# Maxima of the grouped-query scores from the keys' high parts, two stretches of keys at once in the two halves of TensorE's rows

## The chip, the cores and the metric

One Trainium2 chip, one of its cores. The metric is device time in microseconds of one execution of the whole program, two layers of it. The kernel before was timed in 3 runs.

## What is computed

Two layers of a token mixer over 256 context and 2048 latent tokens. Each layer projects the normalised input and runs four branches side by side: A differential attention (two softmax maps per head), B grouped-query attention, C a chunked gating MLP, D gated linear attention; the gated results go through one output projection. The change touches branch B alone: 4 query heads of width 64 share 2 key and value heads.

```python
def gqa_core(q, k, v):
    s = jnp.einsum('bqhgd,bkhd->bhgqk', q, k).astype(jnp.float32) * (GQ_HD ** -0.5)
    p = jax.nn.softmax(s, axis=-1)
    return jnp.einsum('bhgqk,bkhd->bqhgd', p.astype(v.dtype), v)
```

The latent queries read all 2304 keys. The context queries, in the first layer only, read the 256 context keys.

## The kernel before

**Stages.** In each layer the projections for A and B come first, then those of C and D with D's scans, then the attention of A and B together with the gates' projection, then the output projection. Only the attention (lines 789 to 1124) is touched.

**Split operands.** Queries and keys of both attentions lie in DRAM as a high and a low part, so that two or three products of the fast format give nearly the product of full precision. For B the tile `ka` (line 840) holds the 64 rows of a key head's high part interleaved with the 64 of its low part, and `kb` (line 843) the high part again in partitions 0 to 63 and ones in 64 to 127, written by GpSimd. On the query's side `qa` (line 871) holds each row of the high part twice, and `qb` (line 873) the low part in partitions 0 to 63 and, in 64 to 127, what is added to every score of a query: the negated maximum of its row. One product of `ka` with `qa` and one of `kb` with `qb` then give the score less the maximum.

**Blocks.** A block is 256 latent queries (two tiles `qt` of 128) of head r in both A and B; there are 32 in a layer. Keys are cut into 3 chunks of 768. A block makes 12 chunks of A's scores (`da_chunk`, line 901: two matmuls of 384 columns into the two banks of a tile `s`, of which there are two), which VectorE copies out with a running minimum (line 906). Then come the 6 chunks of B's maxima (`g_chunk`, lines 937 to 949): two matmuls of 384 columns (line 940), all 128 rows of `qa` against `ka`, and a pass of VectorE (line 945) that keeps only the running minimum of the negated scores, in the end in column 64 of a zeroed tile `mz`. `qb()` (line 951) transposes `mz` and ScalarE copies 64 partitions of it into `qb`. After that B's scores are computed once more, transposed (`gs`, lines 974 and 975), and go through the exponential into `gp` (line 977). `tr` (line 962) transposes A's weights into `wt`. `pvm` (line 996) multiplies both with the values: `gp` into output partitions 64 to 127, `wt` into 0 to 63, so that the two matmuls of a pair use different halves of TensorE's columns. These come in three groups a block.

**Order.** TensorE's order is the program's own. Every piece of a block has a slot and a priority (`S.at`, lines 1031 to 1071), and `S.run` writes the pieces out slot by slot. The second half of a block (`tr`, `gs`, `pvm`, `o1` to `o3`) lies in the slots of the next block's chunks. Into every slot `pace.fill` puts some matmuls of the gates' projection (`pz`, line 1161), by count, not by time. In a slot the order is: chunk, `tr`, `pace.fill`, `gs`, `pvm`, `pace.fill`.

**Loads.** All loads are issued by SyncE in the program's order. `ld_ka` loads `ka` and then `kb` for one chunk of keys (lines 841 and 844), for every second head; `qload` loads a block's queries, `qa` and `qb` among them (lines 872 and 876).

Of the kernel before, what the change touches and what calls it, by code (L numbers as in the profile page):

```python
# [9 lines left out]
F32 = mybir.dt.float32  # L10
# [10 lines left out]
P = 128  # L21
# [83 lines left out]
class Kernel:  # L105
# [683 lines left out]
    def attention(self, i, out):  # L789
        tc, nc, D = self.tc, self.nc, self.D[i]  # L790
# [8 lines left out]
        with ExitStack() as cx:  # L799
# [6 lines left out]
            sp = cx.enter_context(self.pool(f"sp{i}", 4))  # L806
# [3 lines left out]
            mz = []  # L810
# [8 lines left out]
            def rows(name, r0, cs, dims):  # L819

                a = D[name][r0, 0, cs]
                return bass.AP(tensor=a.tensor, offset=a.offset, ap=[[d * NT, n] for d, n in dims] + [list(a.ap[-1])])
# [12 lines left out]
            def ld_ka(R, c):  # L835
                if R["h"] % 2:
                    return
                r0 = 256 + 64 * (R["h"] // 2)
                cs = slice(c * CH, (c + 1) * CH)
                t = kp.tile([P, CH], F32R, name="ka", tag="ka", bufs=4)  # L840
                nc.sync.dma_start(out=t.bitcast(F32), in_=rows("bqk", r0, cs, [(1, 128)]))
                R["KA"].append(t)
                t = kp.tile([P, CH], F32R, name="kb", tag="kb", bufs=4)
                nc.sync.dma_start(out=t[0:64, :].bitcast(F32), in_=rows("bqk", r0, cs, [(2, 64)]))
                nc.gpsimd.memset(t[64:128, :].bitcast(F32), 1.0)
                R["KB"].append(t)

            def ld_v(R, b):
# [7 lines left out]
            def new_round(r, prev):  # L856
                if r % 2:
                    return dict(h=r, dak=[[], []], V=[], KA=prev["KA"], KB=prev["KB"])
                return dict(h=r, dak=[[], []], V=[], KA=[], KB=[])

            def qload(R, q0):
                h = R["h"]
                ctx = "c" if q0 == 0 else ""
                bufs = 1 if q0 == 0 else 3
                qs = slice(q0, q0 + 256)
                daq = []
                for m in range(2):
                    t = qp.tile([P, 256], F32R, name=f"daq{m}", tag=f"daq{m}{ctx}", bufs=bufs)
                    nc.sync.dma_start(out=t.bitcast(F32), in_=rows("aqk", (2 * h + m) * 32, qs, [(0, 2), (1, 64)]))
                    daq.append(t)  # L870
                QA = qp.tile([P, 256], F32R, name="qa", tag="qa" + ctx, bufs=bufs)
                nc.sync.dma_start(out=QA.bitcast(F32), in_=rows("bqk", h * 64, qs, [(2, 64), (0, 2)]))
                QB = qp.tile([P, 256], F32R, name="qb", tag="qb" + ctx, bufs=bufs)
                a = D["bqk"][h * 64, 1, qs]
                src = bass.AP(tensor=a.tensor, offset=a.offset, ap=[[2 * NT, 64], list(a.ap[-1])])
                nc.sync.dma_start(out=QB[0:64, :].bitcast(F32), in_=src)
                return dict(daq=daq, QA=QA, QB=QB)

            def block(R, Q, q0, nk, base):
                full = nk == NT  # L880
                ch = CH if full else nk
                nch = NCH if full else 1
                hc = ch // 2
                nkt = nk // P
                nu = nkt // 2
                h = R["h"]
# [49 lines left out]

                def g_chunk(qt, c):
                    s = pf.tile([P, 2, 512], F32, name="s", tag="s")
                    for u in range(2):
                        nc.tensor.matmul(  # L940
                            s[:, u, :hc], lhsT=Q["QA"][:, qt * P : (qt + 1) * P],
                            rhs=R["KA"][c][:, u * hc : (u + 1) * hc], start=True, stop=True,
                        )
                    nm = sp.tile([P, 1], F32, name="gm", tag="gm", bufs=6) if c < nch - 1 else mz[qt][:, 64:65]
                    nc.vector.tensor_scalar(  # L945
                        out=junk[:, :ch].rearrange("p (u f) -> p u f", u=2), in0=s[:, :, :hc], scalar1=-1.0,
                        scalar2=GM.get(qt, BIG), op0=ALU.mult, op1=ALU.min, accum_out=nm,
                    )
                    GM[qt] = nm

                def qb():
                    t = pb.tile([P, 512], F32, name="b", tag="b")
                    for qt in range(2):
                        nc.tensor.transpose(t[:, qt * P : (qt + 1) * P], mz[qt], ident)
                    nc.scalar.copy(Q["QB"][64:128, :], t[64:128, :256])

                def tr(u):
                    s = pb.tile([P, 512], F32, name="b", tag="b")
# [72 lines left out]
                s, step = (base, 1) if full else (base + 0.25, 2)  # L1031
# [12 lines left out]
                for c in range(nch):  # L1044
                    for qt in range(2):
                        S.at(s, lambda qt=qt, c=c: g_chunk(qt, c), 0)
                        s += step
                S.at(s + 1, qb, 8)
                b0 = s + 2
                if full:  # L1050
# [26 lines left out]
            base = 0  # L1077
            R = new_round(0, None)
            Qs = {0: qload(R, blocks[0][1])}
            for c in range(NCH):  # L1080
                ld_dak(R, c)
            ld_ka(R, 0)
            pace.begin()
            for c in range(1, NCH):
                ld_ka(R, c)
            for c in range(2):
                S.at(6 + 4 * c, lambda c=c, R=R: ld_v(R, c), 8)
            for bi, (r, q0) in enumerate(blocks):
                if with_ctx and bi % 8 == 0:
                    block(R, qload(R, 0), 0, NCTX, base)  # L1090
                end = block(R, Qs[bi], q0, NT, base)
                Rx = R
                if bi + 1 < len(blocks):
                    if blocks[bi + 1][0] != r:
                        Rx = new_round(r + 1, R)
                        for c, z in enumerate((-14, -10, -8)):
                            S.at(end + z, lambda c=c, Rx=Rx: ld_dak(Rx, c), 8)
                        for c, z in enumerate((-8, 8, 13.5)):
                            S.at(end + z, lambda c=c, Rx=Rx: ld_ka(Rx, c), 8)
                        for c, z in enumerate((-8, 18)):  # L1100
                            S.at(end + z, lambda c=c, Rx=Rx: ld_v(Rx, c), 8)

                    def pre(bi=bi, Rx=Rx):
                        Qs[bi + 1] = qload(Rx, blocks[bi + 1][1])

                    S.at(base + 1, pre, 8)
                S.run(end)
                R = Rx
                base = end
# [355 lines left out]
```

## Time and profile before

| what | value |
|---|---|
| median of 3 runs | 3940.55 us (3936.79 to 3941.91) |
| profiled execution, its own time | 3940.16 us |
| its span, first to last instruction | 3938.4 us |
| PE busy | 3687.3 us (94%) |
| PE weight loads busy | 3078.7 us (78%) |
| VectorE (DVE) busy | 2675.3 us (68%) |
| ScalarE (ACT) busy | 2212.4 us (56%) |
| GpSimd (POOL) busy | 1171.5 us (30%) |
| granted TensorE clock, mean | 0.970 |

PE is TensorE's matmul side and PEld its weight loads, which run beside the matmuls. A matmul's recorded duration reaches from its start to the end of its way through the array; matmuls behind one another overlap, so what one costs is the distance from its start to the next one's. A granted clock of 1.00 is 2.4 GHz, 0.5 is 1.2 GHz.

### The profile page before, as it was taken

What the parts mean: (1) busy time and instruction counts of PE and PEld (TensorE: products, weight loads), DVE (VectorE), ACT (ScalarE), POOL (GpSimd) and SP (SyncE); (2) the same over time, 40 slices, a digit from 0 to 9 for tenths busy, and PEclk for the clock granted to TensorE, in tenths of its full rate; (3) what the DMA queues carried; (4) which work ended last, traced back from release to release, by engine and by line L of the source; (5) the groups of instructions that cost most, each with busy time, mean ns of one, the idle gap of its engine ahead of it and who ended that gap; (6) DMA issues with size and microseconds to landing.
All of it is one profiled execution on the core that took longest, in us unless ns stands there. A gap on an engine that the chain in (4) does not pass through costs nothing.

```text
span 3938.4 us, 71719 instructions
## 1 busy us (share of the span) xinstructions
PE 3687.3 (94%) x25908; PEld 3078.7 (78%) x25908; DVE 2675.3 (68%) x6264; ACT 2212.4 (56%) x4508; POOL 1171.5 (30%) x1328
## 2 busy tenths in 40 slices
PE   7999997999998999998989999979999999999798
PEld 4888885787887888876778878868878778888576
DVE  5555444887787877866666544458777778887575
ACT  4433443666666666665544434436666666666564
POOL 0223222233333333333312222213333333333332
PEclk8999998999999999999999999989999999999899
DMA  7655444534335343326556542254342432432443
GB/s 272 198 172 179 139 151 127 154 107 135 111 100 151 104 121 101 104 85 225 183 178 206 177 144 91 93 142 123 96 138 91 126 115 92 121 100 87 147 163 117
DMA packets 407524, 537.73 MB, mean 137 GB/s; under 512 B 107832, under 2 KB 271616, under 8 KB 407168
## 3 DMA queue, kind: packets, MB, share of 16 engines
q1 hardware_dynamic: 407168, 533.14, 43.1%
q8 instruction: 205, 3.36, 0.4%
q14 instruction: 151, 1.24, 0.1%
HBM read 395.63 MB, written 137.32 MB: 135 GB/s over the span
## 4 chain that ended last, share of the span: by engine, by line
PE 74%; DVE 9%; DMA 7%; ACT 5%; issue 3%; SPq 1%; POOL 1%; DVEq 0%; ACTq 0%; POOLq 0%
PE pv L996 12%; PE pz L1161 8%; PE b L962 6%; PE s L901 6%; PE b L974 4%; PE s L940 3%; PE b L975 3%; PE po L139 2%; PE po L141 2%; PE po L140 2%; DVE e L906 2%; PE pc L139 2%; PE pc L140 2%; PE pc L141 2%; DVE e L932 1%
## 5 line engine op out<-in xcount | busy, mean ns | idle before, releaser
L985 POOL TENSOR_TENSOR acc<-acc,gp 128x512 f32<-128x512 f32 x448 | 578.2, 1291 | 955.0 <-ACT gp L977 950.0
L915 ACT ACTIVATE e<-e,dm 128x1152 f32<-128x1152 f32 x512 | 642.1, 1255 | 157.8 <-DVE e L906 155.2
L906 DVE TENSOR_SCALAR_CACHE_REDUCE e<-s,dm 128x768 f32<-128x768 f32 x512 | 515.3, 1016 | 310.0 <-PE s L901 306.7
L1161 PE MATMUL pz<-fw,fh 128*128 128x256 f32 x3264 | 711.4, 303 | 10.5 <-DMA fh<-hs 6.0
L1161 PEld LDWEIGHTS pz<-fw,fh 128*128 128x128 f32 x3264 | 528.5, 194 | 54.7 <-issue 45.7
L996 PE MATMUL pv<-wt,v 128*64 128x256 f32 x2320 | 548.4, 386 | 0.0
L996 PE MATMUL pv<-gp,v 128*64 128x256 f32 x2320 | 548.4, 386 | 0.0
L977 ACT ACTIVATE gp<-b 128x512 f32<-128x512 f32 x580 | 345.5, 596 | 361.1 <-PE b L975 341.1
L901 PE MATMUL s<-dak,daq 128*128 128x384 f32 x1568 | 421.5, 351 | 43.4 <-DMA dak<-aqk 18.7
L996 PEld LDWEIGHTS pv<-gp,v 128*64 128x64 f32 x2320 | 304.2, 138 | 173.0 <-issue 18.9
L966 ACT COPY wt<-b 128x512 f32<-128x512 f32 x580 | 340.5, 587 | 154.0 <-PE b L962 151.3
L932 DVE SCALAR_TENSOR_TENSOR e<-e,r,e 128x576 f32<-128x576 f32 x512 | 396.4, 825 | 3.4
L974 PE MATMUL b<-qa,ka 128*128 128x256 f32 x1160 | 318.3, 296 | 53.9 <-ACT gp L977 29.0
L962 PE MATMUL b<-ident,e 128*128 128x128 f32 x2304 | 355.1, 277 | 7.0 <-ACT gp L977 2.5
L975 PE MATMUL b<-qb,kb 128*128 128x256 f32 x1160 | 304.8, 284 | 0.0
L996 PEld LDWEIGHTS pv<-wt,v 128*64 128x64 f32 x2320 | 304.2, 138 | 0.0
L962 PEld LDWEIGHTS b<-ident,e 128*128 128x128 f32 x2304 | 275.5, 142 | 32.4 <-ACT gp L977 11.9
L901 PEld LDWEIGHTS s<-dak,daq 128*128 128x128 f32 x1568 | 247.7, 195 | 53.1 <-issue 20.2
L974 PEld LDWEIGHTS b<-qa,ka 128*128 128x128 f32 x1160 | 221.2, 191 | 78.8 <-ACT gp L977 37.7
L945 DVE TENSOR_SCALAR_CACHE_REDUCE junk<-s,gm 128x768 bf16<-128x768 f32 x256 | 259.7, 1015 | 30.3 <-PE s L940 15.7
L906 DVE TENSOR_SCALAR_CACHE_REDUCE e<-s 128x768 f32<-128x768 f32 x256 | 243.2, 956 | 41.9 <-PE s L901 33.0
L940 PE MATMUL s<-ka,qa 128*128 128x384 f32 (+1 forms) x784 | 216.7, 358 | 19.1 <-DMA ka<-bqk 7.3
(300 smaller groups left out, 8100.4 us busy)
## 6 DMA issues: line engine op xcount, KB each, us to landing
fh<-hs SPq DMA_DIRECT2D x272, 512.0 KB
hs<-hh SPq DMA_DIRECT2D x36, 512.0 KB
hs<-hl SPq DMA_DIRECT2D x36, 512.0 KB
hh<-hs SPq DMA_DIRECT2D x36, 512.0 KB
hl<-hs SPq DMA_DIRECT2D x36, 512.0 KB
dak<-aqk SPq DMA_DIRECT2D x96, 192.0 KB
daq<-aqk SPq DMA_DIRECT2D x136, 128.0 KB
z<-zs SPq DMA_DIRECT2D x136, 128.0 KB
```

The lines of the kernel that those rows point to most:

```text
L901: nc.tensor.matmul(s[:, u, :hc], lhsT=Q["daq"][m][:, qt * P : (qt + 1) * P], rhs=R["dak"][m][c][:, u * hc : (u + 1) * hc], start=True, sto ...
L906: nc.vector.tensor_scalar(out=E[qt, m][:, c * ch : (c + 1) * ch].rearrange("p (u f) -> p u f", u=2), in0=s[:, :, :hc], scalar1=-SC, scalar ...
L915: nc.scalar.activation(e, e, AF.Exp, bias=NM[qt, m], scale=-1.0, accum_out=L[qt][:, b, m : m + 1])
L932: nc.vector.scalar_tensor_tensor(out=E0[:, a : a + w], in0=E1[:, a : a + w], scalar=RR[qt][:, 3:4], in1=E0[:, a : a + w], op0=ALU.mult, op ...
L962: nc.tensor.transpose(s[:, j * 256 + qt * P : j * 256 + (qt + 1) * P], W[qt][:, k * P : (k + 1) * P], ident)
L966: nc.scalar.copy(WT[u], s)
L974: nc.tensor.matmul(o, lhsT=R["KA"][k // 6][:, ks], rhs=Q["QA"], start=True, stop=False)
L975: nc.tensor.matmul(o, lhsT=R["KB"][k // 6][:, ks], rhs=Q["QB"], start=False, stop=True)
L977: nc.scalar.activation(g, s, AF.Exp, scale=0.125)
L985: nc.gpsimd.tensor_tensor(out=B["acc"], in0=B["acc"], in1=g, op=ALU.add)
L996: nc.tensor.matmul(B["pv"][o : o + 64, :256], lhsT=R["V"][k // VH][:, k % VH, o : o + 64], rhs=x[:, js], start=k == 0, stop=k == nkt - 1,)
L1161: nc.tensor.matmul(ps[:, :256], lhsT=h[:, a, k % 4], rhs=w[:, b], start=k == 0 and z == 0, stop=k == KT - 1 and z == 2)
```

## The change

`ka` now holds the high part in partitions 0 to 63 and the low part in 64 to 127; `qa` holds the high part twice, whole. `kb` and `qb` change halves: ones and the negated maximum lie in partitions 0 to 63, the keys' high part and the queries' low part in 64 to 127. A chunk of maxima is computed from the high parts alone: the first matmul takes the lower 64 partitions of `qa` and of `ka`, the second the upper 64 of `qa` and of `kb`, each for its own 384 keys and its own bank. The maximum goes to column 0 of `mz`. What `gs` multiplies is the same as before.

```diff
@@ ld_ka
-                nc.sync.dma_start(out=t.bitcast(F32), in_=rows("bqk", r0, cs, [(1, 128)]))
+                nc.sync.dma_start(out=t.bitcast(F32), in_=rows("bqk", r0, cs, [(1, 2), (2, 64)]))
                 R["KA"].append(t)
                 t = kp.tile([P, CH], F32R, name="kb", tag="kb", bufs=4)
-                nc.sync.dma_start(out=t[0:64, :].bitcast(F32), in_=rows("bqk", r0, cs, [(2, 64)]))
-                nc.gpsimd.memset(t[64:128, :].bitcast(F32), 1.0)
+                nc.sync.dma_start(out=t[64:128, :].bitcast(F32), in_=rows("bqk", r0, cs, [(2, 64)]))
+                nc.gpsimd.memset(t[0:64, :].bitcast(F32), 1.0)
                 R["KB"].append(t)
@@ qload
                 QA = qp.tile([P, 256], F32R, name="qa", tag="qa" + ctx, bufs=bufs)
-                nc.sync.dma_start(out=QA.bitcast(F32), in_=rows("bqk", h * 64, qs, [(2, 64), (0, 2)]))
+                nc.sync.dma_start(out=QA.bitcast(F32), in_=rows("bqk", h * 64, qs, [(0, 2), (2, 64)]))
                 QB = qp.tile([P, 256], F32R, name="qb", tag="qb" + ctx, bufs=bufs)
...
-                nc.sync.dma_start(out=QB[0:64, :].bitcast(F32), in_=src)
+                nc.sync.dma_start(out=QB[64:128, :].bitcast(F32), in_=src)
@@ block
                 def g_chunk(qt, c):
                     s = pf.tile([P, 2, 512], F32, name="s", tag="s")
-                    for u in range(2):
+
+                    for u, K in ((0, R["KA"]), (1, R["KB"])):
+                        d = slice(64 * u, 64 * u + 64)
                         nc.tensor.matmul(
-                            s[:, u, :hc], lhsT=Q["QA"][:, qt * P : (qt + 1) * P],
-                            rhs=R["KA"][c][:, u * hc : (u + 1) * hc], start=True, stop=True,
+                            s[:, u, :hc], lhsT=Q["QA"][d, qt * P : (qt + 1) * P],
+                            rhs=K[c][d, u * hc : (u + 1) * hc], start=True, stop=True,
                         )
-                    nm = sp.tile([P, 1], F32, name="gm", tag="gm", bufs=6) if c < nch - 1 else mz[qt][:, 64:65]
+                    nm = sp.tile([P, 1], F32, name="gm", tag="gm", bufs=6) if c < nch - 1 else mz[qt][:, 0:1]
...
                         nc.tensor.transpose(t[:, qt * P : (qt + 1) * P], mz[qt], ident)
-                    nc.scalar.copy(Q["QB"][64:128, :], t[64:128, :256])
+                    nc.scalar.copy(Q["QB"][0:64, :], t[0:64, :256])
```

## Rows read from the trace of the kernel before

**Rows 1.** The page, part 1: busy time, share of the span, instructions of each engine.
```profile
PE 3687.3 (94%) x25908; PEld 3078.7 (78%) x25908; DVE 2675.3 (68%) x6264; ACT 2212.4 (56%) x4508; POOL 1171.5 (30%) x1328
```

**Rows 2.** Windows, busy time by engine: both attentions, one block, its stretch of maxima.
```profile
core 0: us, PE busy (x) PEld busy (x) DVE busy (x) ACT busy (x) POOL busy (x), PEclk, DMA share, GB/s
700.00:1690.00 990.00, 953.02 (x7251) 809.43 (x7252) 788.06 (x1637) 653.14 (x1197) 328.58 (x269) 0.99 0.39 117
2640.00:3640.00 1000.00, 953.83 (x7242) 813.58 (x7243) 793.52 (x1644) 664.17 (x1197) 338.14 (x275) 0.98 0.37 109
...
3240.00:3271.20 31.20, 30.47 (x238) 26.01 (x237) 25.07 (x53) 21.23 (x39) 11.02 (x10) 1.00 0.31 96
...
3259.97:3269.24 9.27, 9.27 (x73) 7.62 (x71) 8.71 (x19) 5.50 (x10) 3.86 (x3) 1.00 0.24 73
```

**Rows 3.** The chain of waits in that block: start us, us, what.
```profile
3260.13 0.35 PE s L940 x2
...
3261.27 0.48 PE s L940 x2
...
3262.93 0.44 PE b L962 x4
...
3265.14 0.61 PE b L962 x4
...
3266.10 2.74 PE pv L996 x24
3268.84 0.56 PE s L940 x2
```

**Rows 4.** Instruction groups: B's maxima on TensorE (the page) and on VectorE (by tile).
```profile
L940 PE MATMUL s<-ka,qa 128*128 128x384 f32 (+1 forms) x784 | 216.7, 358 | 19.1 <-DMA ka<-bqk 7.3
...
L945 DVE TENSOR_SCALAR_CACHE_REDUCE junk<-s,gm x256: 995/1017/1021, 705.4 to 3649.7; 128x768 bf16<-128x768 f32 x128
...
L945 DVE TENSOR_SCALAR_CACHE_REDUCE junk<-s x136: 412/954/959, 697.4 to 3641.9; 128x768 bf16<-128x768 f32 x128, 128x256 bf16<-128x256 f32 x8
```

**Rows 5.** Timeline of TensorE's matmuls into a group of `pvm`: start us, us, instruction.
```profile
3265.50 0.60 PE L1161 MATMUL pz<-fw,fh 128*128 128x256 f32 x3
3266.03 0.43 PE L996 MATMUL pv<-gp,v 128*64 128x256 f32 x1
3266.04 0.43 PE L996 MATMUL pv<-wt,v 128*64 128x256 f32 x1
3266.30 0.38 PE L996 MATMUL pv<-gp,v 128*64 128x256 f32 x1
...
3266.51 0.38 PE L996 MATMUL pv<-gp,v 128*64 128x256 f32 x1
```

**Rows 6.** Timeline of the weight loads, for a chunk amid others and one behind `pvm`.
```profile
3263.32 0.31 PEld L940 LDWEIGHTS s<-ka,qa 128*128 128x128 f32 x2
...
3268.77 0.30 PEld L940 LDWEIGHTS s<-ka,qa 128*128 128x128 f32 x2 [0.38 <-issue]
```

**Rows 7.** Timeline of TensorE around a matmul of 98 rows, in the projections of D.
```profile
363.23 0.39 PE L141 MATMUL pc<-cwh,hl 128*128 128x512 f32 x1
363.46 0.28 PE L588 MATMUL g<-w,rT 98*128 98x256 f32 x1
363.58 0.39 PE L139 MATMUL pc<-cwh,hh 128*128 128x512 f32 x1
```

**Rows 8.** Waits of TensorE, whole span: waiter, releaser: us in total, times, longest us.
```profile
PE b L974 <- ACT wt L966: 24.2, 42, 1.0
...
PE s L940 <- DMA ka<-bqk: 7.3, 2, 3.9
PE s L940 <- DVE e L906: 6.0, 20, 0.6
```

**Rows 9.** SyncE's issues of the key loads, by tile: duration ns min/median/max, first and last start.
```profile
L841 SPq DMA_DIRECT2D ka<-bqk x12: 326/397/957, 656.0 to 3162.5; - x12
...
L844 SPq DMA_DIRECT2D kb<-bqk x12: 450/483/602, 658.7 to 3163.5; - x12
```

## The prediction

> **What bounds the kernel now.** I read the busy shares first: TensorE is busy 94% of the span and no other engine more than 78% [rows 1]. A share over the whole span says little about one stage, so next come the windows. In the two attention stages TensorE is busy 953 of 990 and 954 of 1000 us, VectorE 788 and 794 [rows 2]. In one undisturbed block of 31.2 us the figures are 30.47 and 25.07, at a granted clock of 1.00, the 2.4 GHz level. In its stretch of maxima, 3259.97 to 3269.24, TensorE is busy all of 9.27 us and VectorE 8.71: here VectorE is a close second. The chain of waits settles who decides. In that stretch it runs over TensorE alone [rows 3], and TensorE waits for VectorE ahead of the maxima for 6.0 us in the whole program [rows 8]. So what TensorE gains or loses there is nearly what the kernel gains or loses, with little slack from VectorE either way.
>
> **How often.** Line 940 has 784 matmuls, so 392 pairs; VectorE's 256 and 136 passes make the same 392, of which 8 are the short ones of the context queries [rows 4]. The other 384 are 6 in each of the 64 blocks. A pair costs 0.35 us from its start to the next instruction's [rows 3], 0.175 a matmul.
>
> **What the change removes.** The two matmuls of a pair now use different halves of the array's rows and different banks. The trace has no such pair, but it has the same thing across columns: the `gp` and `wt` matmuls of line 996 start 0.01 us apart, and the pair takes no longer than its period of 0.21 [rows 5]. If rows behave as columns do, one of the two 0.175 goes: 384 x 0.175 = 67 us at most. At least, nothing goes.
>
> **What it adds.** A matmul on 64 rows stands between matmuls on the full array, so the shape in which the array is used changes twice a pair. The nearest rows for the price are those around `pvm`, the only shape change in the attention. Going in: the steady period of a pair is 0.21 (3266.30 to 3266.51), the first pair takes 0.27 (3266.03 to 3266.30), which is 0.06 more [rows 5]. With what lies ahead of it, the chain has the whole: 24 matmuls are 12 pairs, 12 x 0.216 (0.21 and the 0.01 between a pair's starts) is 2.59, the group takes 2.74, so **0.15 going in** [rows 3]. Coming out: the maxima's pair right behind `pvm` takes 0.56 instead of 0.35, **0.21 coming out** [rows 3]. The weight loads show why. Amid full-array work the pair's loads start at 3263.32, ahead of the matmuls they serve; behind `pvm` the loads sit idle 0.38 us "issue" and start at 3268.77, with nothing to wait for [rows 6]. The array is run empty first, and then the first load, normally hidden, lies bare. Going in to `pvm` a bare load of 64 columns cost the 0.06 above; the maxima load 128 columns, by which I estimate 0.06 more. A pair in the midst of full-array work would thus pay 0.15 + 0.06 + 0.21 = 0.42, or an estimated 0.36 where the next instruction hides part of its own bare load. Less the 0.175 saved, that is 0.18 to 0.24 **more** per pair; I take 0.21.
>
> Does a change in rows alone cost this? The 98-row matmul of line 588 does not: it starts 0.23 after its predecessor and its successor 0.12 after it, the plain spacings [rows 7]. But 98 rows need the full height, so this row leaves the question open. The bounds are therefore 0 and 0.42 a pair. I take the upper one, since the rows of `pvm` are the only ones where the array is used in parts and then whole, and there the price is the same each time.
>
> The Trainium skill, TensorEngine Tiling (Array Packing), Key Properties, has the rule that speaks against the change: changing the tiling mode, and not just the tile, drains TensorE, with row tilings among the modes. The trace shows that for column tiles only; by the rule the sum is the one below, without it that of the first rival.
>
> **The sum.** One pair of the six stands right behind `pvm` [rows 3]. It pays 0.21 already; changed, it still pays that, saves 0.175 and pays 0.21 for the way back: +0.03. The block gets 5 x 0.21 + 0.03 = 1.08 us longer on TensorE. Some of that fills waits: one pair in the stretch takes 0.48 instead of 0.35, one set of transposes 0.61 instead of 0.44 [rows 3]. Both are short waits for others that vanish if TensorE comes later: -0.30. That leaves 0.78 a block, 64 x 0.78 = 50 us.
>
> **The rest.** Same number and sizes of loads, of the fill with ones on GpSimd, of ScalarE's 64-partition copy and of the transposes: zero. They all run beside TensorE, which has 30.47 of 31.2 us to cover them. A chunk's second matmul now needs `kb`, issued behind `ka` on SyncE. Twice the maxima wait for `ka`, 7.3 us in all [rows 8]; one issue more of about 0.48 us [rows 9] each time makes 1 us, at most 2. The matmuls queued behind it wait with it.
>
> Against the profiled execution's 3940.2 us (span 3938.4, and 0.4 under the median of the runs): 3940.2 + 50 + 1 = 3991, rounded down to **3990 us**. Its own range: at 0.24 and with no wait filled, 1.23 x 64 = 79, 4019. At 0.18 with the 0.30 filled, 0.63 x 64 = 40, 3980; the 24 us that `gs` waits for ScalarE [rows 8] may be filled too, which makes 3957.
>
> **Rivals.**
> *Faster: the shape change in rows is free.* For it: the price was seen for columns alone. Against it: the pattern of [rows 3] and [rows 6]. Then 6 x 0.175 = 1.05 us a block is saved on TensorE, but VectorE has 8.71 busy in the 9.27 us of the stretch [rows 2], so no more than 0.56 comes out before VectorE decides: 64 x 0.56 = 36 us, 3904. If later stretches give back what VectorE holds, up to 67, 3873. It decides from the point where the price of both changes of shape falls under 0.175.
> *Slower still: price paid and no overlap.* If the halves run one after the other, the 0.175 is not saved: 5 x 0.39 + 0.21 - 0.30 = 1.9 us a block, 4060. If only the second weight load follows the first, 0.11 x 6 x 64 = 42 more, 4032. Against it: the pair of line 996, which overlaps in loads and matmuls.
> *The halves do not act as parts.* Row halves count as the full array with fewer rows, as in [rows 7], run behind one another and cost nothing: 3940. A price on one of the two ways alone lands near there as well: 0.15 to 0.27 against 0.175.
>
> **Chances.** Forecast 0.60, free change 0.20, slower still 0.09, no parts or half the price 0.11. The bound between faster, same and slower is 0.2%, 8 us, about what a measurement of this kernel can tell from no change. Faster: 0.20 and a quarter of the last, 0.23. Same: half of the last and the edges of the others, 0.08. Slower: 0.69. The range reaches from the forecast's upper end, 4019, down through no change to 3895, over half of the free case: 0.60 + 0.11 + 0.12 = 0.83. The likeliest case alone: 3957 to 4019.
>
> **What would show it.** Right: the second matmul of line 940 starts within 0.02 us of the first; ahead of the pair and behind it PEld sits idle some 0.1 to 0.2 us on "issue"; the chain shows a pair at 0.5 to 0.6 us and the block at about 32.0 us instead of 31.2; VectorE waits more for line 940. Wrong towards faster: weight loads of the pair start while the matmul before still runs, the pair takes about 0.18, and the stretch ends with VectorE in the chain. Wrong towards no change: the pair's starts are 0.175 apart with no idle. If a pair costs the extra 0.2 and the block still takes 31.2 us, the step that failed is that the chain runs over TensorE alone. A granted clock in the attention under 0.98 would be a cost that I have at nothing.

## The result and the profile after

The changed kernel takes 4060.69 us (median of 4 runs, 4053.31 to 4063.23) against 3939.36 before: a ratio of 1.0307, 95% interval 1.0295 to 1.0319, 121 us slower. The forecast had the direction, but 50 us of the 121, and the range ended at 4019.

First the page of the kernel after, part 1, against [rows 1]:

```profile
PE 3739.2 (92%) x25908; PEld 3029.7 (75%) x25908; DVE 2682.6 (66%) x6264; ACT 2209.1 (54%) x4508; POOL 1170.4 (29%) x1328
```

TensorE's share has fallen while the span grew: it waits more than before. Two things are mixed here, and two views part them. The first is the timeline of an undisturbed block of the second layer: ScalarE's copy `ot` comes once a block, so the distance between two of them is a block's time. Before the change, and then after:

```profile
3248.27 0.35 ACT L1003 COPY ot<-pv 128x256 f32<-128x256 f32 x1
3279.46 0.35 ACT L1003 COPY ot<-pv 128x256 f32<-128x256 f32 x1
```

```profile
3366.55 0.35 ACT L1005 COPY ot<-pv 128x256 f32<-128x256 f32 x1
3398.41 0.35 ACT L1005 COPY ot<-pv 128x256 f32<-128x256 f32 x1
```

A block went from 31.19 to 31.86 us. That is 0.67 more, where the prediction had 0.78; taken for all 64 blocks it makes 43 us. The other 78 are not in the undisturbed blocks. They show in the second view, the waits of TensorE in the whole span (waiter, releaser: us in total, times, longest us); before, and then after:

```profile
PE s L901 <- DMA dak<-aqk: 18.7, 5, 8.6
PE s L901 <- DMA daq<-aqk: 16.8, 2, 16.3
...
PE pz L1161 <- DMA fh<-hs: 6.0, 4, 3.9
```

```profile
PE s L901 <- DMA dak<-aqk: 32.0, 5, 15.4
PE s L901 <- DMA daq<-aqk: 29.3, 2, 28.8
PE s L942 <- DMA ka<-bqk: 28.9, 2, 14.5
PE pz L1163 <- DMA fh<-hs: 27.3, 8, 8.1
```

With `ka` at 7.3 before [rows 8], TensorE waits 69 us longer for these four (13.3 + 12.5 + 21.6 + 21.3). Three of them are loads that the change does not touch. They fall where an attention begins and where the third round, the first head with new keys for B, loads them. By the last `ot` the kernel after is 124 us behind; from `ot` to `ot`, five places hold 94 of these: the way to the first block (24), the block after it (12), the stretch between the two attentions (33) and one block in the third round of each layer (14 and 11). In that block of the first layer the windows from one `ot` to the next, before and then after, show what the wait brings with it (the columns are those of [rows 2], the granted clock third from the end):

```profile
1220.20:1260.30 40.10, 36.15 (x263) 29.84 (x262) 27.05 (x61) 24.05 (x47) 13.21 (x12) 0.96 0.46 130
```

```profile
1262.80:1317.33 54.53, 39.09 (x264) 29.85 (x263) 27.14 (x61) 23.79 (x47) 13.75 (x12) 0.84 0.32 96
```

The block takes 14.4 us more. The wait for `ka` in it grew from 3.4 to 14.3, and TensorE's busy time by 2.9 for the same work: 0.7 of it comes with the new shape, as in an undisturbed block (30.47 to 31.13), and the rest goes with a granted clock of 0.84 instead of 0.96.

**The halves, as they ran.** The timeline of TensorE's matmuls in the kernel after, around the first pair of a block's maxima, and then the chain of waits in the same stretch, beside [rows 3]:

```profile
3378.11 0.28 PE L1163 MATMUL pz<-fw,fh 128*128 128x256 f32 x1
3378.32 0.44 PE L942 MATMUL s<-ka,qa 64*128 64x384 f32 x1
3378.32 0.44 PE L942 MATMUL s<-kb,qa 64*128 64x384 f32 x1
3378.70 0.66 PE L964 MATMUL b<-ident,e 128*128 128x128 f32 x4
```

```profile
3381.10 0.37 PE s L942 x2
3381.47 0.59 PE b L964 x4
...
3382.30 0.38 PE s L942 x2
3382.68 0.43 PE pz L1163 x2
...
3385.01 2.74 PE pv L998 x24
3387.75 0.38 PE s L942 x2
3388.13 0.32 PE pz L1163
```

The two halves start together, so the overlap is real. The matmul ahead of them starts at 3378.11 and the pair at 3378.32: 0.21, where 0.12 is the plain spacing. That is the way into the new shape. The weight loads show both ways: after the load of `pz` PEld sits idle 0.19 us until the pair's two loads start together, and again 0.19 behind them.

```profile
3377.94 0.19 PEld L1163 LDWEIGHTS pz<-fw,fh 128*128 128x128 f32 x1
3378.32 0.18 PEld L942 LDWEIGHTS s<-ka,qa 64*128 64x128 f32 x1 [0.19 <-issue]
3378.32 0.18 PEld L942 LDWEIGHTS s<-kb,qa 64*128 64x128 f32 x1
...
3382.60 0.30 PEld L1163 LDWEIGHTS pz<-fw,fh 128*128 128x128 f32 x2 [0.19 <-issue]
```

So the way out shows in the chain not in the pair's own 0.37 (the prediction looked for 0.5 to 0.6 there) but in whatever follows, whose first weight load lies bare: transposes take 0.59 instead of the 0.44 of [rows 3], two `pz` 0.43 instead of the 0.24 (two plain spacings of 0.12). A pair with transposes behind it costs 0.37 + 0.59 against 0.35 + 0.44, so 0.17 more; with `pz` behind it, 0.38 + 0.43 against 0.35 + 0.24, 0.22 more. The prediction said 0.18 to 0.24. The two short waits that [rows 3] show in the stretch, 0.13 and 0.17, are gone, as the prediction had it.

**The loads.** Now SyncE's own line at the start of the first attention: start us, us, DMA issue. Before, and then after:

```profile
676.46 0.42 SPq L841 DMA_DIRECT2D ka<-bqk  x1
676.94 0.45 SPq L844 DMA_DIRECT2D kb<-bqk  x1
677.43 1.09 SPq L869 DMA_DIRECT2D daq<-aqk  x2
678.56 2.30 SPq L872 DMA_DIRECT2D qa<-bqk  x1
680.91 0.60 SPq L876 DMA_DIRECT2D qb<-bqk  x1
```

```profile
684.58 0.53 SPq L841 DMA_DIRECT2D ka<-bqk  x1
685.16 3.62 SPq L844 DMA_DIRECT2D kb<-bqk  x1
688.82 8.32 SPq L869 DMA_DIRECT2D daq<-aqk  x2
697.19 3.68 SPq L872 DMA_DIRECT2D qa<-bqk  x1
700.91 2.69 SPq L876 DMA_DIRECT2D qb<-bqk  x1
```

After `ka`, everything behind it in the queue waits, up to 8.32 us for a pair of issues that took 1.09. A window of this stretch says why (DMA share and GB/s last):

```profile
692.00:702.00 10.00, 0.00 (x0) 0.00 (x0) 0.79 (x2) 0.77 (x2) 0.00 (x0) 0.50 0.13 50
```

The DMA share is the mean over 16 engines: 0.13 is two of them, at 50 GB/s together, while TensorE does nothing at all and its granted clock is 0.50, the 1.2 GHz level. In `ka` and `qa` as changed, the outermost dimension of the transfer, the first pair in its list of dimensions, is 2 (`(1, 2)` and `(0, 2)`); before it was 128 and 64. At 50 GB/s, by estimate, the 384 KB of a `ka` take 7.9 us and the 128 KB of a `qa` 2.6.

The Trainium skill, DMA: Bandwidth & Descriptors, Rules for kernel authors, states this: the slowest dimension that is not 1 sets how many engines carry a transfer, so that a leading broadcast of c copies, with c under 16, confines it to at most c of them. The window above agrees, with 0.13 for c = 2.

### The profile page after: what moved, and what is told of

It is laid out like the page before. It is cut to its first block, busy times and chain, and to the rows that moved or that the text cites. A ratio compares the mean times of both kernels' runs of the same rounds, so it can differ in the third digit from the quotient of the medians.

```text
span 4061.4 us, 71718 instructions
## 1 busy us (share of the span) xinstructions
PE 3739.2 (92%) x25908; PEld 3029.7 (75%) x25908; DVE 2682.6 (66%) x6264; ACT 2209.1 (54%) x4508; POOL 1170.4 (29%) x1328
## 4 chain that ended last, share of the span: by engine, by line
PE 74%; DMA 9%; DVE 6%; ACT 5%; issue 3%; SPq 2%; POOL 1%; DVEq 0%; ACTq 0%; POOLq 0%
PE pv L998 12%; PE pz L1163 9%; PE b L964 6%; PE s L901 5%; PE b L976 4%; PE s L942 3%; PE b L977 3%; PE po L139 2%; PE po L141 2%; PE po L140 2%; DMA fh<-hs 2%; PE pc L139 1%; PE pc L140 1%; PE pc L141 1%; DVE e L906 1%
## 5 line engine op out<-in xcount | busy, mean ns | idle before, releaser
L1163 PE MATMUL pz<-fw,fh 128*128 128x256 f32 x3264 | 733.1, 310 | 42.3 <-DMA fh<-hs 27.3
L964 PE MATMUL b<-ident,e 128*128 128x128 f32 x2304 | 364.8, 281 | 6.3 <-ACT gp L979 2.5
L964 PEld LDWEIGHTS b<-ident,e 128*128 128x128 f32 x2304 | 263.7, 142 | 53.2 <-ACT gp L979 18.0
L977 PEld LDWEIGHTS b<-qb,kb 128*128 128x128 f32 x1160 | 222.0, 191 | 0.0
```

The lines of the kernel that those rows point to most:

```text
L964: nc.tensor.transpose(s[:, j * 256 + qt * P : j * 256 + (qt + 1) * P], W[qt][:, k * P : (k + 1) * P], ident)
L977: nc.tensor.matmul(o, lhsT=R["KB"][k // 6][:, ks], rhs=Q["QB"], start=False, stop=True)
L1163: nc.tensor.matmul(ps[:, :256], lhsT=h[:, a, k % 4], rhs=w[:, b], start=k == 0 and z == 0, stop=k == KT - 1 and z == 2)
```

## The experiments

Theory A was that there are two separate costs, the array's shape in the blocks and the two loads at the starts. Theory B was that all of it is TensorE's and the waits for DMA only show work queued behind it. The kernel before took 3937.38, 3937.31 and 3937.14 us beside the three groups of runs.

**Loads of 64 rows.** The changed kernel; `ka` and `qa` each in two transfers, outermost dimension 64:

```diff
-nc.sync.dma_start(out=t.bitcast(F32), in_=rows("bqk", r0, cs, [(1, 2), (2, 64)]))
+for z in range(2):
+    src = rows("bqk", r0, cs, [(2, 64)])
+    src = bass.AP(tensor=src.tensor, offset=src.offset + z * NT, ap=src.ap)
+    nc.sync.dma_start(out=t[64 * z : 64 * z + 64, :].bitcast(F32), in_=src)
...
-nc.sync.dma_start(out=QA.bitcast(F32), in_=rows("bqk", h * 64, qs, [(0, 2), (2, 64)]))
+for z in range(2):
+    nc.sync.dma_start(out=QA[64 * z : 64 * z + 64, :].bitcast(F32), in_=rows("bqk", h * 64, qs, [(2, 64)]))
```

> The changed kernel with one thing undone: ka and qa are each loaded by two transfers of 64 rows, so that no transfer's outermost dimension is 2. Theory A (two separate costs): the change of the array's shape costs 0.68 us in each of 64 blocks, 44 us, and the rest of the 121 us comes from ka and qa arriving late at the start of each attention and of the third round. Then this takes about 3983 us (3975 to 3995), and the DMA share while ka is loaded goes from about 0.13 to near 1. Theory B (one cost): all of it is TensorE's, and the waits for DMA at those places only show work that was queued behind a later TensorE. Then this stays at 4050 to 4065 us.

Measured: 3977.7 us, ratio 1.0106 (1.0089 to 1.0123), 40 us over the kernel before and 83 under the changed one. The wait for `daq` in it:

```profile
PE s L905 <- DMA daq<-aqk: 20.7, 2, 20.3
```

Theory A holds, and theory B falls. The expectation of a DMA share near 1 was too strong: SyncE issues its loads at the same place in 676 to 690 at a share of 0.44. `daq` stands among them, with its outermost dimension of 2; more on it below.

**The loads alone.** The changed kernel with the maxima on all 128 rows:

```diff
-for u, K in ((0, R["KA"]), (1, R["KB"])):
-    d = slice(64 * u, 64 * u + 64)
+for u in range(2):
     nc.tensor.matmul(
-        s[:, u, :hc], lhsT=Q["QA"][d, qt * P : (qt + 1) * P],
-        rhs=K[c][d, u * hc : (u + 1) * hc], start=True, stop=True,
+        s[:, u, :hc], lhsT=Q["QA"][:, qt * P : (qt + 1) * P],
+        rhs=R["KA"][c][:, u * hc : (u + 1) * hc], start=True, stop=True,
     )
```

> The changed kernel's loads and halves, but the maxima computed as before, on all 128 rows of qa and ka (the array keeps its full shape). Theory A: the loads alone cost the other part, 121 - 44 = 77 us: 4016 us (4000 to 4030), with blocks of 31.2 us in the second layer as in the kernel before. Theory B: the loads cost nothing, 3935 to 3945 us.

Measured: 4025.05 us, ratio 1.0226 (1.0211 to 1.0241), 88 us over the kernel before. Its blocks are those of the kernel before (31.20 us), its waits those of the changed one:

```profile
3302.29 0.35 ACT L1004 COPY ot<-pv 128x256 f32<-128x256 f32 x1
3333.49 0.35 ACT L1004 COPY ot<-pv 128x256 f32<-128x256 f32 x1
```

```profile
PE s L901 <- DMA dak<-aqk: 31.2, 5, 14.6
PE s L941 <- DMA ka<-bqk: 30.3, 2, 15.2
PE s L901 <- DMA daq<-aqk: 29.3, 2, 28.7
```

So the two costs stand apart and nearly add: 40 + 88 = 128 against 121.

**Which load.** The changed kernel with one of the two loads above in 64 rows and the other left at an outermost dimension of 2; first `ka` alone, then `qa` alone (the diff is the half of the first one that names it).

> The changed kernel with ka alone in loads of 64 rows; qa keeps its outermost dimension of 2. Splits the cost of the loads (changed kernel less the kernel with both in 64 rows: about 83 us against 3978). Theory: ka is the larger, 384 KB a load and 6 loads an attention, against 128 KB for qa: most of the 83 us goes, 3990 to 4020 us. Rival: qa, which stands in SyncE's queue right behind daq, itself on two DMA engines, is what holds up the rest: 4030 us or more.

> The changed kernel with qa alone in loads of 64 rows; ka keeps its outermost dimension of 2. Theory (ka is the larger part): 4020 to 4045 us. Rival (qa holds up the rest): under 4010 us.

Measured: 3996.08 us (ratio 1.0150, 1.0133 to 1.0167) with `ka` mended, 4039.85 (1.0258, 1.0243 to 1.0273) with `qa` mended. `ka` is 65 us of the loads' cost, `qa` 21, and together they make about the 83 of both.

**What the overlap is worth.** The first experiment's kernel with both matmuls of a pair in the same half:

```diff
-for u, K in ((0, R["KA"]), (1, R["KB"])):
-    d = slice(64 * u, 64 * u + 64)
+for u in range(2):
+    d = slice(0, 64)
...
-        rhs=K[c][d, u * hc : (u + 1) * hc], start=True, stop=True,
+        rhs=R["KA"][c][d, u * hc : (u + 1) * hc], start=True, stop=True,
```

> As the first of these kernels, but both matmuls of a pair take the lower 64 partitions of qa and ka, so that they cannot overlap; the maxima are the same numbers. Measures what the overlap is worth. Theory A: the overlap is real and worth the 0.16 us of one matmul per pair where TensorE decides, 384 x 0.16 = 61 us over the first of these kernels (40 to 65 over). Rival: the pair's time is set by emptying the array and bare weight loads, and the second matmul is hidden under them: within 10 us of the first of these kernels.

Measured: 4032.3 us, ratio 1.0242 (1.0226 to 1.0257), 55 us over the first experiment. In its chain of waits the pair takes 0.55, where the overlapped one has 0.37, and the block 32.91 us:

```profile
3330.39 0.55 PE s L946 x2
3330.93 0.59 PE b L968 x4
```

```profile
3318.54 0.35 ACT L1009 COPY ot<-pv 128x256 f32<-128x256 f32 x1
3351.45 0.35 ACT L1009 COPY ot<-pv 128x256 f32<-128x256 f32 x1
```

The overlap thus saves what a matmul costs, 0.18 a pair. The two changes of shape cost more than that.

**The same cause in the kernel before.** `daq` had an outermost dimension of 2 all along:

```diff
-nc.sync.dma_start(out=t.bitcast(F32), in_=rows("aqk", (2 * h + m) * 32, qs, [(0, 2), (1, 64)]))
+for z in range(2):
+    nc.sync.dma_start(out=t[64 * z : 64 * z + 64, :].bitcast(F32), in_=rows("aqk", (2 * h + m) * 32, qs, [(1, 64)]))
```

> The kernel before, with one thing changed that the change did not touch: daq, whose outermost dimension of 2 was there already, is loaded by two transfers of 64 rows. Theory A, in which a transfer's outermost dimension decides how many DMA engines carry it: the waits for daq (16.8 us) and part of those queued behind it go, 3905 to 3930 us. Theory B: no difference, 3935 to 3945 us.

Measured: 3895.45 us, ratio 0.9896 (0.9881 to 0.9911). This is 42 us under the kernel before, the fastest of all that ran, and more than expected. The wait for `daq` itself hardly went (16.0 us are left, once). The gain lies in the blocks in which the next head's loads are issued: from `ot` to `ot`, eight of these blocks hold 36 of the 45 us by which the last `ot` comes earlier, and the stretch between the two attentions 6. The windows of one such block, in the kernel before and in this one:

```profile
910.60:951.70 41.10, 34.94 (x246) 29.33 (x245) 30.98 (x69) 24.81 (x52) 11.37 (x9) 0.92 0.58 168
```

```profile
909.70:944.40 34.70, 32.43 (x246) 27.12 (x246) 30.74 (x69) 24.98 (x52) 11.40 (x9) 1.00 0.69 193
```

The same work takes 6.4 us less, at a DMA share of 0.69 instead of 0.58 and a granted clock of 1.00 instead of 0.92. Of the 6.4, 3.9 are time in which TensorE was idle (6.2 us before, 2.3 now) and 2.5 are the same matmuls running faster. The waits in the two windows show the path, first in the kernel before and then in this one:

```profile
ACT fw L127 <- DMA fs<-in_w_in_dram: 7.7, 1, 7.7
PE b L974 <- ACT gp L977: 4.0, 1, 4.0
```

```profile
ACT fw L127 <- DMA fs<-in_w_in_dram: 2.7, 1, 2.7
```

ScalarE waits for `fs`, weights of the gates' projection issued behind `daq`, its work on `gp` stands behind that, and TensorE waits for `gp`. With `daq` in 64 rows `fs` comes earlier and the 4.0 us are gone. How the 42 part into idle time and clock over the whole run was not taken apart.

**Maxima behind `pvm`.** If the price is the change of shape, the pairs belong where the shape changes anyway. Two pairs behind each of the three groups of `pvm`; with the loads of the first experiment, then with `daq` mended too, and then the latter with maxima on 128 rows:

```diff
-S.at(s, lambda qt=qt, c=c: g_chunk(qt, c), 0)
+S.at(base + 4.6 + 6 * c + 0.1 * qt if full else s, lambda qt=qt, c=c: g_chunk(qt, c), 0)
```

> The first of the kernels (ka and qa in loads of 64 rows, halves as changed), with the chunks of maxima moved: two pairs right behind each of the three groups of pvm in a block, with nothing between them, where the array's shape changes anyway. Theory A (what a pair pays is the number of changes of shape): of the six ways in and out a block keeps three extra ways out of 0.21 us, against 6 x 0.175 = 1.05 saved, so a block is 0.42 us shorter than the kernel before's: 30.8 us, 27 us less in all than before, 3905 to 3920 us. Rival (VectorE or the dependences of the new order decide): the block stays at 31.2 us or goes over it, 3935 us or more.

> The kernel with the chunks of maxima behind pvm, and daq in two loads of 64 rows as well. Theory A: the gain of daq's loads (42 us) comes on top: about 3870 us (3860 to 3885). Rival: the two gains overlap, 3895 us or more.

> As the kernel just named, chunks of maxima in the same new places, but each computed on all 128 rows as in the kernel before. Separates the place from the halves. Theory A: the place alone gives nothing, as the array's shape changes as often as before: 3895 us (3885 to 3905), 20 to 35 us more than with the halves. Rival: the place is what gains, by an evener load on VectorE, and this comes within 8 us of the kernel with the halves.

Measured: 4094.07 us (ratio 1.0398, 1.0384 to 1.0412), 4052.35 (1.0296, 1.0282 to 1.0310) and 4059.44 (1.0313, 1.0299 to 1.0327). The remedy failed. The place costs more than the shape ever did: with the loads and halves of the first experiment it adds 116 us (4094 against 3978), and on 128 rows 164 to the 3895 of the maxima in their old slots (there the loads of `ka` and `qa` differ too). The waits of the first of the three, and a piece of its chain, show the turn:

```profile
PE s L905 <- DVE junk L951: 136.4, 119, 5.6
```

```profile
3412.17 3.00 DVE e L936 x4
3415.17 0.95 DVE junk L951 x2
...
3416.17 0.62 PE s L905 x2
```

VectorE's passes over the maxima now stand behind its four long combinations of A's weights, the two tiles `s` stay taken, and A's next chunk waits. VectorE, which has 25 of 31 us of work a block, decides as soon as its order is wrong. The halves gained 7 us there (4052 against 4059) where 20 to 35 were expected, since TensorE no longer decided.

## Why the prediction failed, and where it was right

**What bounds the kernel: right in the blocks.** There the time went with TensorE's, 0.67 us for a computed 0.78. One reading was short: ahead of the maxima TensorE waited for VectorE not 6.0 us but 11.0 (another 5.0 for `junk`), which does not change the sum.

**What the change removes: right.** The halves overlap, and same-half matmuls cost 55 us more (40 to 65 was expected from 384 x 0.16).

**What it adds: right in kind and nearly in size.** Row halves pay for the change of shape as column halves do. Taken alone the step is worth 40 us, measured; the prediction had 50. The pair behind `pvm` adds 0.02 (0.38 + 0.32 against 0.56 + 0.12), where 0.03 was computed. In the sum for `pvm` the 0.216 is the period itself (ten take from 3266.30 to 3268.46), not 0.21 and a gap of 0.01; the value stands. The rule of the Trainium skill that the prediction weighed (TensorEngine Tiling (Array Packing), Key Properties), that a changed tiling mode drains TensorE, now has rows for row tilings as well: the 0.21 ahead of the pair and the bare load behind it.

**The rest: this step failed.** "Same number and sizes of loads", hence zero, was 83 us. It counted bytes and transfers, not how a transfer is spread. The reason given, that TensorE's 30.47 of 31.2 us cover the loads, holds in an undisturbed block, not at the start of an attention or of the third round, where TensorE stands still until the load lands. The diff showed an outermost dimension of 2 in `ka` and `qa`, and the trace of before held the price: `daq`, with the same leading 2, has SyncE stand at the issues behind it (the 2.30 us of `qa` against 0.60 for `qb` above). The rows of the prediction have only the key loads of SyncE's line [rows 9]. The wait for `ka`, put at 1 us more for one more issue of `kb`, became 21.6 more for `ka`'s own transfer. The clock, which the prediction had at nothing, is part of the price: the whole program's mean fell from 0.970 to 0.962, and in the block of the third round above some 2 of the 14.4 us go with it.

**A rival that hit the number for another reason.** "Slower still: price paid and no overlap" gave 4060, and 4061 was measured. But the halves start together, so that is not what happened. A time that fits does not show a mechanism.

## What to carry to other kernels

Rearranging a load so that a broadcast or a split into halves leads its access pattern can leave it on 2 of 16 DMA engines: write one transfer per half, with many rows outermost, and look for such loads in what was there before (here worth 42 us). A matmul on half the rows amid full-array matmuls saves one matmul and pays two changes of shape, 0.18 us against some 0.38 (the 0.17 to 0.22 that were lost and the 0.18 saved). By estimate from these figures it needs at least three pairs in a row to gain; no run here had that many. And before a piece of work is moved, ask which engine stands behind it: here two score tiles tied TensorE to VectorE's order.

## What was not expected of the hardware

Two row halves of 64 start in the same 0.01 us, as column halves do. A transfer with a leading dimension of 2 ran at 50 GB/s and held up the later issues of its queue, up to 8.32 us for two. And a load that TensorE does not wait for can cost it time through the loads behind it: in the block shown for `daq`, 4.0 us of waiting for ScalarE and 2.5 us of the same matmuls at a granted clock of 0.92 instead of 1.00.
